# RWKV-7 and forgetting-attention layer: one recurrence operation for two heads, scores in quadrants, the inverse placed by 0/1 columns, and lo parts on VectorE

## Chip, cores and metric

The kernel runs on one core of one Trainium2 chip. The metric is the device time of one execution in microseconds, as the median of three runs. The engines are TensorE (PE in the profile, with its weight loads as PEld), VectorE (DVE), ScalarE (ACT), GpSimd (POOL) and SyncE (SP), which issues most of the DMAs.

## What is computed

One layer over 528 tokens (16 learned ones and 512 of the input) with 1024 channels. One projection of the normed input feeds three users: eight heads of the RWKV-7 delta rule, eight heads of forgetting attention, and two gates.

```python
u = rmsnorm(h, norm_mix[l])
proj = u @ w_in[l]
...
y_rw = rwkv7_branch(feat_rw, ...)   # S_t = S_{t-1} (diag(w_t) + a_t^T b_t) + v_t^T k_t ;  y_t = S_t r_t
y_fx = fox_branch(feat_fx, ...)     # softmax(q k^T * scale + F_q - F_k, causal) v
merged = gates[..., :D_MODEL] * (y_rw @ w_out_rw[l]) + gates[..., D_MODEL:] * (y_fx @ w_out_fx[l])
h = h + (merged @ w_o[l]).astype(h.dtype)
z = rmsnorm(h, norm_mlp[l])
h = h + (jnp.square(jax.nn.relu(z @ w_up[l])) @ w_down[l]).astype(h.dtype)
```

## The kernel before

**Products in two parts.** Large matrices are multiplied in three passes. Each 128 x 512 float32 weight block `wraw` is split into `whi`, a cast to float32r by ACT, and `wlo`, the difference `wraw - whi`. PE then forms hi*hi, hi*lo and lo*hi into one accumulator.

**Stages.** From the start to about 45 us the input is normed and the small projections run. From there to about 462 us run, interleaved, the 40 remaining blocks of the input projection (`projections`, matmuls L497), the recurrence (`Pair`, `inverse`, `chain`, `group_norm`) and attention (`fox_features`, `attention`). Then follow the output projections and the MLP. The change lies in the interleaved stage.

**Order of the work.** In that stage PE's order is written by a planner. `Turns` holds streams (Python generators) with ranks: 0 for `chain`, 1 for `recurrent`, 2 for `attention`, 3 for `fox_features`, 4 for `group_norm`, 8 for `projections`. A stream yields a time at which its operands are due; the first in rank whose due time plus a reserve (`ROOM`, 0.0 us for rank 0 and 0.8 for rank 1) is reached gets PE next, and `projections` fills what is left. Due times come from `Clock`, which books every instruction on its engine at a fixed price plus a rate per column (DVE 0.18 us + 1.06 ns, POOL 0.30 us + 2.1 ns). The order of DVE, ACT and POOL is made by the framework's scheduler from program order and priorities; each engine then works its list in that order. So PE stands still where an operand is later than the planner thought.

**Projections.** `convert` (L459) splits the next two halves of a weight block while the current one is multiplied. The cast is L466 on ACT, the difference L467 is on DVE for the first two blocks and on POOL after that. `wraw`, `whi` and `wlo` have four buffers each.

**The recurrence.** The eight heads are handled as four pairs; a pair's two heads lie on partitions 0-63 and 64-127 (`hss`). Two pairs make a group. Time is cut into 9 chunks of 64.

- `rows` builds for each head e a tile `L[e]` of 128 x 9 x 128. On the head's own 64 partitions stand the removal rows (columns 0-63: -kkn times the decay P, L753, and the first column of each chunk, L754) and the read rows (columns 64-127: r times P, L755).
- `scores` multiplies, per chunk and head, two of the three blocks of `BK` (b, k and a copy of b) with L (L784): weights of 64 x 128, so one matmul gives b's scores on the head's own 64 partitions and k's scores on the other 64. Every three chunks two PSUM banks (one for each head) are filled; DVE masks them into `Bm` (L787, own partitions) and into the other half of `L[e]` (L788).
- `inverse` inverts unit triangular 64 x 64 matrices: the 32 x 32 diagonal blocks of `Bm` are gathered into `Ain` by copies per partition quadrant (L821), transposed in blocks of 32, solved over 15 steps on DVE, transposed back, and placed by copies per quadrant (L845) into `Tt` and `Dn`, whose other 32 x 32 blocks are zeroed by POOL (L816, L840). Products of `Bm`, `Dn`, `W2` and `Tt` on PE (L851, 64 x 64 quadrants, both heads in one bank) complete it.
- `chain` then goes through the chunks: PE L911 gives Rs (copied by DVE L913), PE L917 with `Tt` gives the corrections (DVE L919), PE L932 the new state (DVE L934), PE L940 and L943 the outputs.
- `group_norm` (L221 and its neighbours are a reciprocal square root on 128 x 8) ends a half.

## Time and profile before

| | us |
|---|---|
| median of three runs | 889.76 (888.0 to 890.99) |
| the profiled execution | 888.58 |
| its span, first to last instruction | 886.8 |
| PE busy | 856.2 |
| DVE busy | 626.4 |
| ACT busy | 452.3 |
| POOL busy | 229.4, of which L467 has 103.7 in 76 operations |

A line of the profile names the source line, the engine, the operation, the tiles it writes and reads, the shape and the count; then come times, and in brackets or after a bar the idle time of the engine before it and what ended that. A busy PE is not PE at its peak, since matmuls are pipelined: two that start 0.23 us apart each show 0.39 us. The granted clock is TensorE's; 0.50 means that it ran at half speed.

### The profile page before, as it was taken

The page shows a single profiled execution, that of the slowest core. Times are in us where ns is not written, and L with a number is a line of the kernel's source. Part 1 is how long each engine was busy: PE and PEld are TensorE (multiplying, and loading weights), DVE is VectorE, ACT ScalarE, POOL GpSimd, SP SyncE. Part 2 cuts the span into 40 slices and gives each one's busy share as a digit, 9 for nine tenths or more (in the row PEclk, how much of TensorE's full clock was granted, in tenths as well). Part 3 has the DMA queues.
Part 4 walks back from the last instruction along what each step waited for, and adds up shares of the span by engine and source line. Part 5 has one row for each costly group of instructions (what it writes and reads, how often), then busy time and mean ns, then how long its engine had stood idle before and what let it go on. Part 6 is the DMA issues. An engine that isn't in the chain of part 4 may idle for free.

```text
span 886.8 us, 15663 instructions
## 1 busy us (share of the span) xinstructions
PE 856.2 (97%) x5896; PEld 698.0 (79%) x5896; DVE 626.4 (71%) x1186; ACT 452.3 (51%) x935; POOL 229.4 (26%) x201
## 2 busy tenths in 40 slices
PE   7889899999999999999989999999999999999998
PEld 6878887778896777677858788988888888888886
DVE  7975895547877883564377665587687777877787
ACT  7737333865465533665365563366445434544452
POOL 1154443222353351213102200210630171046000
PEclk9999999999999999999979999999999999999999
DMA  6121114021111231121256650472564175327331
GB/s 216 60 86 48 50 50 139 2 86 60 51 62 49 68 128 61 61 74 49 72 207 202 205 174 21 131 217 68 177 204 115 50 232 163 106 73 230 113 96 71
DMA packets 51339, 95.90 MB, mean 108 GB/s; under 512 B 5816, under 2 KB 6968, under 8 KB 51264
## 3 DMA queue, kind: packets, MB, share of 16 engines
q1 hardware_dynamic: 47680, 86.52, 30.4%
q0 software_dynamic: 1280, 4.20, 1.5%
q10 hardware_dynamic: 2304, 4.20, 1.3%
q8 instruction: 46, 0.75, 0.3%
q14 instruction: 29, 0.24, 0.1%
HBM read 88.57 MB, written 6.31 MB: 107 GB/s over the span
## 4 chain that ended last, share of the span: by engine, by line
PE 76%; DVE 11%; ACT 3%; DMA 3%; issue 2%; POOL 0%; ACTq 0%; DVEq 0%; POOLq 0%
PE pj L497 20%; PE po L1143 20%; PE po L1261 11%; PE pd L1261 5%; PE po L1113 3%; PE po L1064 2%; PE pw L851 1%; DMA gl<-gd 1%; PE psc L603 1%; PE py L648 1%; PE psr L784 1%; DVE L L755 1%; PE pbt L799 1%; PE pssq L549 1%; PE ppt L634 1%
## 5 line engine op out<-in xcount | busy, mean ns | idle before, releaser
L497 PE MATMUL pj<-uhi,whi 128*128 128x264 f32 (+1 forms) x480 | 167.6, 349 | 0.0
L497 PE MATMUL pj<-ulo,whi 128*128 128x264 f32 (+1 forms) x480 | 156.0, 325 | 2.4 <-DVE ulo L400 2.4
L497 PE MATMUL pj<-uhi,wlo 128*128 128x264 f32 (+1 forms) x480 | 155.6, 324 | 0.0
L467 POOL TENSOR_TENSOR wlo<-wraw,whi 128x512 fp32r<-128x512 f32 x76 | 103.7, 1368 | 194.9 <-ACT whi L466 180.8
L497 PEld LDWEIGHTS pj<-uhi,whi 128*128 128x128 f32 x480 | 91.6, 191 | 20.4 <-issue 11.3
L497 PEld LDWEIGHTS pj<-ulo,whi 128*128 128x128 f32 x480 | 92.1, 192 | 7.3 <-DVE ulo L400 3.0
L497 PEld LDWEIGHTS pj<-uhi,wlo 128*128 128x128 f32 x480 | 91.9, 191 | 7.1
L1143 PE MATMUL po<-zlo,whi 128*128 128x512 f32 (+1 forms) x248 | 94.9, 383 | 0.0
L1143 PE MATMUL po<-zhi,whi 128*128 128x512 f32 (+1 forms) x248 | 94.8, 382 | 0.0
L1143 PE MATMUL po<-zhi,wlo 128*128 128x512 f32 (+1 forms) x248 | 94.8, 382 | 0.0
L235 DVE TENSOR_TENSOR wlo<-wraw,whi 128x512 fp32r<-128x512 f32 x88 | 74.4, 856 | 27.8 <-ACT whi L234 27.7
L234 ACT CAST whi<-wraw 128x512 fp32r<-128x512 f32 x88 | 53.5, 617 | 48.3 <-DMA wraw<-in_wup 20.2
L1189 POOL TENSOR_TENSOR t<-traw 128x512 f32<-128x512 f32 x24 | 34.2, 1433 | 155.3 <-DVE wlo L270 138.9
L466 ACT CAST whi<-wraw 128x512 fp32r<-128x512 f32 x80 | 48.9, 617 | 42.0 <-PE pj L497 23.3
L1261 PE MATMUL po<-wlo,fhi 128*128 128x512 f32 x160 | 62.8, 392 | 0.2 <-DVE wlo L270 0.2
L270 DVE TENSOR_TENSOR wlo<-t,whi 128x512 fp32r<-128x512 f32 x64 | 49.4, 784 | 18.9 <-ACT whi L269 18.0
L269 ACT CAST whi<-t 128x512 fp32r<-128x512 f32 x64 | 39.9, 623 | 44.5 <-DVE wlo L270 20.6
L1261 PE MATMUL po<-whi,flo 128*128 128x512 f32 x160 | 62.4, 390 | 0.0
L1261 PE MATMUL po<-whi,fhi 128*128 128x512 f32 x160 | 62.0, 389 | 0.0
L1143 PEld LDWEIGHTS po<-zhi,wlo 128*128 128x128 f32 x248 | 46.6, 188 | 9.1
L1143 PEld LDWEIGHTS po<-zhi,whi 128*128 128x128 f32 x248 | 46.6, 188 | 9.1
L1143 PEld LDWEIGHTS po<-zlo,whi 128*128 128x128 f32 x248 | 46.6, 188 | 8.9
(298 smaller groups left out, 1839.7 us busy)
## 6 DMA issues: line engine op xcount, KB each, us to landing
wraw<-in_win SPq DMA_DIRECT2D x84, 256.0 KB, 2.6
wraw<-in_wup SPq DMA_DIRECT2D x64, 256.0 KB, 3.3
wraw<-in_wdn SPq DMA_DIRECT2D x48, 256.0 KB, 2.6
traw<-in_wdn SPq DMA_DIRECT2D x48, 256.0 KB, 3.0
gd<-gt ACTq DMA_DIRECT2D x16, 256.0 KB, 2.0
wraw<-in_wout SPq DMA_DIRECT2D x16, 256.0 KB, 3.0
gl<-gd SPq DMA_DIRECT2D x16, 256.0 KB, 3.0
wraw<-in_wo SPq DMA_DIRECT2D x16, 256.0 KB, 3.0
```

The lines of the kernel that those rows point to most:

```text
L234: A.copy(hi, raw)
L235: low.tensor_tensor(lo, raw, hi.bitcast(F32), ALU.subtract)
L269: A.copy(hi, x)
L270: V.tensor_tensor(lo, x, hi.bitcast(F32), ALU.subtract)
L466: A.copy(hi, raw)
L467: low.tensor_tensor(lo, raw, hi.bitcast(F32), ALU.subtract)
L497: mm(po, a, b[:, k, a0:a1], start=n == 0, stop=n == 23)
L1064: mm(po, a, b[:, k, :], start=n == 0, stop=n == 11)
L1113: mm(po, a[:, k, 128 * i:128 * i + 128], b[:, k, :], start=n == 0, stop=n == 23)
L1143: mm(po[:, t0:t1], a, b[:, k, t0:t1], start=n == 0, stop=n == 23)
L1189: eng.tensor_tensor(t, sums[c, pair] if c in (T1, T2) else c, d, ALU.add)
L1261: mm(x[i], a[:, k, left, 128 * i:128 * i + 128], c, start=start and k == 0 and n == 0, stop=stop and k == n_pairs - 1 and n == 2)
```

## The change

- `rows`: L753, L754 and L755 run once over all 128 partitions into `L[0]`; ACT copies the second head's partitions from there to `L[1]`, in two copies.
- `scores`: for each chunk, four matmuls with 64 x 64 weights instead of two with 64 x 128. The first bank takes the b scores of both heads, each on its own partitions; the second takes the k scores of both, each on the other head's partitions. `Bm` is masked in one operation on 128 partitions, `L` in two on 64.
- `inverse`: a tile `even` of two 0/1 columns marks the even and odd quadrants of 32 partitions. `Ain` is formed as `Bm`'s left block times the first column plus its right block times the second; `Tt` and `Dn` are written in two operations each, source times column. The zeroing of `Tt` and `Dn` by POOL falls away.
- `convert`: the difference `wlo` is always on DVE. `Clock` books whatever is written to a tile named `wlo` on POOL, as before.

```diff
-            eng = str(x.engine).split(".")[-1]
+            eng = "Pool" if out.startswith("wlo") else str(x.engine).split(".")[-1]
...
+    even = cp.tile([128, 2], F32, name="even")
...
+        for qd in range(4):
+            for odd in range(2):
+                G.memset(even[32 * qd:32 * qd + 32, odd:odd + 1], float(qd % 2 == odd))
...
         def convert(job, raws):
-            low = V if len(converted) < 2 else G
+            low = V
...
-                self.L = []
-                for e, hs in enumerate(hss):
-                    l1 = rp.tile([128, NCH, 128], F32, name=f"L{e}", bufs=2)
-                    V.scalar_tensor_tensor(l1[hs, :, 1:64], kkn[hs, :, 1:64], -1.0, P[hs, :, 0:63], ALU.mult, ALU.mult)
-                    V.tensor_scalar(l1[hs, :, 0:1], kkn[hs, :, 0:1], -1.0, None, ALU.mult)
-                    V.tensor_tensor(l1[hs, :, 64:128], r3[hs], P[hs], ALU.mult)
-                    self.L.append(l1)
+                self.L = l0, l1 = [rp.tile([128, NCH, 128], F32, name=f"L{e}", bufs=2) for e in range(2)]
+                V.scalar_tensor_tensor(l0[:, :, 1:64], kkn[:, :, 1:64], -1.0, P[:, :, 0:63], ALU.mult, ALU.mult)
+                V.tensor_scalar(l0[:, :, 0:1], kkn[:, :, 0:1], -1.0, None, ALU.mult)
+                A.copy(l1[hss[1], :, :64], l0[hss[1], :, :64])
+                V.tensor_tensor(l0[:, :, 64:128], r3, P, ALU.mult)
+                A.copy(l1[hss[1], :, 64:], l0[hss[1], :, 64:])
...
-                    sps = [psm("psr").rearrange("p (a b) -> p a b", b=128) for e in range(2)]
+                    sb, sk = [psm("psr").rearrange("p (a b) -> p a b", b=128) for e in range(2)]
                     for j in range(3):
-                        for e, hs in enumerate(hss):
-                            mm(sps[e][:, j, :], BK[hs, c0 + j, e:e + 2, :].rearrange("p a b -> p (a b)"), L[e][hs, c0 + j, :], start=True, stop=True)
-                    for e, hs in enumerate(hss):
-                        os, sp = hss[1 - e], sps[e]
-                        V.tensor_tensor(Bm[hs, c0:c0 + 3, :], sp[hs, :3, :], bc(tmask[hs], 1, 3), ALU.mult)
-                        V.tensor_tensor(L[e][os, c0:c0 + 3, :], sp[os, :3, :], bc(tmask[os], 1, 3), ALU.mult)
+                        for sp, row, turn in ((sb, 0, 1), (sk, 1, -1)):
+                            for (e, hs), os in zip(enumerate(hss), hss[::turn]):
+                                mm(sp[os, j, :], BK[hs, c0 + j, row, :], L[e][hs, c0 + j, :], start=True, stop=True)
+                    V.tensor_tensor(Bm[:, c0:c0 + 3, :], sb[:, :3, :], bc(tmask, 1, 3), ALU.mult)
+                    for e, os in enumerate(hss[::-1]):
+                        V.tensor_tensor(L[e][os, c0:c0 + 3, :], sk[os, :3, :], bc(tmask[os], 1, 3), ALU.mult)
...
-            if g > 0:
-                for r0, r1 in low:
-                    G.memset(Tt[r0, :, :, 32:64], 0.0)
-            for qd in range(4):
-                rs_ = slice(32 * qd, 32 * qd + 32)
-                o = 32 * (qd % 2)
-                for pr_ in range(2):
-                    V.tensor_copy(Ain[rs_, :, NCH * pr_:NCH * pr_ + NCH].rearrange("p t n -> p n t"), Bms[pr_][rs_, :, o:o + 32])
+            for pr_ in range(2):
+                dst = Ain[:, :, NCH * pr_:NCH * pr_ + NCH].rearrange("p t n -> p n t")
+                V.tensor_scalar(dst, Bms[pr_][:, :, :32], even[:, 0:1], None, ALU.mult)
+                V.scalar_tensor_tensor(dst, Bms[pr_][:, :, 32:64], even[:, 1:2], dst, ALU.mult, ALU.add)
...
-            G.memset(Dn, 0.0)
             for dst, src in ((Tt2, TT), (Dn, At)):
-                for qd in range(4):
-                    rs_ = slice(32 * qd, 32 * qd + 32)
-                    o = 32 * (qd % 2)
-                    V.tensor_copy(dst[rs_, :, o:o + 32], src[rs_, :, :n2].rearrange("p t n -> p n t"))
+                for odd in range(2):
+                    V.tensor_scalar(dst[:, :, 32 * odd:32 * odd + 32], src[:, :, :n2].rearrange("p t n -> p n t"), even[:, odd:odd + 1], None, ALU.mult)
```

## The prediction

> **What bounds the kernel now.** I read the page's head first, then the stretches, the waits of PE, the clock, one place in order of time, and last the groups that the diff touches. The page's first lines:

> ```profile
> span 886.8 us, 15663 instructions
> PE 856.2 (97%) x5896; PEld 698.0 (79%) x5896; DVE 626.4 (71%) x1186; ACT 452.3 (51%) x935; POOL 229.4 (26%) x201
> ```

> PE is busy nearly always, so the kernel can gain only where PE waits, runs at half clock, or gets less work. Stretches show where (columns: length, busy of PE, PEld, DVE, ACT, POOL, granted clock, DMA):

> ```profile
> 45.00:440.00 395.00, 380.36 (x3613) 304.80 (x3614) 262.79 (x618) 198.37 (x488) 131.47 (x113) 0.98 0.20 67
> 440.00:462.00 22.00, 18.43 (x116) 12.50 (x117) 18.33 (x53) 14.82 (x39) 0.00 (x0) 0.77 0.45 157
> 462.00:887.00 425.00, 420.07 (x1926) 347.93 (x1924) 307.36 (x429) 204.06 (x338) 92.36 (x72) 1.00 0.45 141
> ```

> The change works in 45 to 440 us only. PE idles 14.6 us there (395.0 - 380.4), with DVE at 67% and POOL at 33%. What it waits for, in total over the kernel:

> ```profile
> PE ppt L632 <- DVE pe L619: 2.8, 4, 1.8
> PE psr L784 <- DVE L L755: 2.7, 2, 1.6
> PE psr L784 <- DVE tm L313: 2.6, 2, 1.3
> PE pw L851 <- DVE AX L845: 1.7, 1, 1.7
> PE pch L917 <- DVE Rs L913: 1.6, 1, 1.6
> PE psr L784 <- DVE BK L743: 1.6, 1, 1.6
> PE psr L784 <- DVE L L788: 1.5, 2, 1.2
> ```

> DVE is what comes late: before the scores (L784), the inverse (L851), the chain (L917). After such waits the clock is halved for a stretch (the 0.50 that stands before the DMA share):

> ```profile
> 60.77:64.18 3.41, 3.41 (x24) 2.76 (x21) 3.33 (x9) 0.00 (x0) 0.94 (x1) 0.50 0.45 153
> 98.31:101.73 3.42, 3.33 (x24) 3.14 (x25) 3.00 (x7) 0.00 (x0) 1.07 (x1) 0.50 0.49 155
> 210.95:214.37 3.42, 3.42 (x22) 3.13 (x20) 1.25 (x4) 1.49 (x4) 1.42 (x1) 0.50 0.01 2
> 330.42:333.83 3.41, 3.41 (x21) 2.15 (x19) 0.00 (x0) 1.21 (x2) 1.27 (x1) 0.50 0.22 79
> 449.89:460.13 10.24, 9.12 (x52) 6.00 (x52) 9.20 (x26) 6.45 (x16) 0.00 (x0) 0.50 0.60 223
> ```

> Each of the first four costs half its length, 1.7 us, 6.8 us together; the fifth is the end of the stage and costs 5.1. Why DVE is late is seen in order of time:

> ```profile
> 207.59 1.27 POOL L467 TENSOR_TENSOR wlo<-wraw,whi 128x512 fp32r<-128x512 f32 x1 [1.38 <-ACT whi L466]
> 207.69 1.19 DVE L221 TENSOR_TENSOR rsgw<-st,rsgy 128x8 f32<-128x8 f32 x1
> ...
> 210.25 0.29 DVE L913 COPY Rs<-pch 128x128 f32<-128x128 f32 x1
> ...
> 210.59 0.45 PE L917 MATMUL pch<-Rs,Tt 64*64 64x64 f32 x8 [1.64 <-DVE Rs L913]
> ```

> An operation on 8 elements takes 1.19 us because it ends with POOL's wlo. Rs stands behind it, PE waits 1.64 us, and the half-clock stretch at 210.95 follows. By line, the same operation has two durations (ns, min/median/max):

> ```profile
> L467 POOL TENSOR_TENSOR wlo<-wraw,whi x76: 1261/1289/1830, 45.0 to 427.6; 128x512 fp32r<-128x512 f32 x76
> L467 DVE TENSOR_TENSOR wlo<-wraw,whi x4: 674/680/694, 25.8 to 42.6; 128x512 fp32r<-128x512 f32 x4
> L221 DVE TENSOR_TENSOR rsgw<-st,rsgy x12: 164/167/1249, 206.5 to 421.6; 128x8 f32<-128x8 f32 x12
> L753 DVE SCALAR_TENSOR_TENSOR L<-okk,P x8: 741/912/1811, 52.4 to 279.8; 64x567 f32<-64x567 f32 x8
> L755 DVE TENSOR_TENSOR L<-orr,P x8: 739/1334/1837, 56.7 to 265.5; 64x576 f32<-64x576 f32 x8
> L821 DVE COPY Ain<-Bm x16: 423/442/1461, 66.8 to 294.9; 32x288 f32<-32x288 f32 x16
> L845 DVE COPY Tt<-TT x8: 649/1188/1766, 128.9 to 321.4; 32x576 f32<-32x576 f32 x8
> L845 DVE COPY AX<-AX x8: 645/1152/1706, 133.4 to 328.2; 32x576 f32<-32x576 f32 x8
> L787 DVE TENSOR_TENSOR Bm<-psr,cs x24: 539/552/560, 61.4 to 291.4; 64x384 f32<-64x384 f32 x24
> ```

> Operations between SBUF tiles stretch by up to the 1.3 us of a wlo; L787, which reads PSUM, never does. The wait under tm L313 is of the same kind; that memset only follows this pair of L755, whose end at 60.27 us is what the scores lacked:

> ```profile
> 56.69 3.58 DVE L755 TENSOR_TENSOR L<-orr,P 64x576 f32<-64x576 f32 x2
> ```

> **The lo parts, wlo to DVE.** 76 operations leave POOL and cost DVE 76 x 0.68 = 51.7 us, by the four that it does already. What it gets back where POOL no longer holds it, median less minimum times count: L753 8 x 0.17, L755 8 x 0.60, L845 8 x 0.54 + 8 x 0.51, L821 16 x 0.02, together 14.9 us; others like L221 come on top. On DVE a wlo takes a turn between the chain's steps, and waits for its cast on ACT with everything behind it: Rs, uv, masks. PE waits for Rs. The planner still books wlo on POOL, so PE's order does not allow for that. No DMA is added or moved; the wraw buffers come free some 0.6 us sooner after each cast, and SP's loads are not what PE waits for.

> **L, the masks, the inverse.** L753 and L755 go from 8 to 4 each: 4 x (0.74 + 0.74) = 5.9 us. The masks (L787, and L788 of the same count and shape) go from 48 to 36 operations: 12 x 0.55 = 6.6. Ain takes 8 operations for 16 (3.5 by 0.44), the placement of Tt and Dn 8 for 16 (5.2 by 0.65). That the new ones, on 128 partitions, last as long as the old on 32 or 64 is an estimate from L467 on 128 and L755 on 64, both near 0.7 us for some 550 elements; with a column as factor and strided reads, from 0.65 (as now) to 1.2 us (the held copies), and I take 0.65. DVE's sum: 262.8 + 51.7 - 14.9 - 21.2 = 278 us of 395; its load hardly moves, so not its load but who holds it decides. POOL's memsets of Tt and Dn go, eight tiny ones come before the stage; POOL is idle, so nothing. ACT gets 8 copies of one head's half of L, by the nearest row:

> ```profile
> L744 ACT COPY BK<-BK x4: 672/672/675, 56.8 to 283.3; 128x576 f32<-128x576 f32 x4
> ```

> at most 8 x 0.67 = 5.4 us, under PE's projections at ACT's 50%; the last lies before the scores of the second head. The path through L still shortens: six operations of 2 x (0.74 + 0.16 + 0.74) = 3.3 us (0.16 for the column, as L221) become 1.64 + 0.67 = 2.3.

> **The scores in quadrants.** 144 matmul records of 64x128 weights become 288 of 64x64, as long each. The rows for how many run at once:

> ```profile
> 64.38 0.94 PE L784 MATMUL psr<-L,BK 64*128 64x128 f32 x12
> ...
> 65.25 0.19 PEld L497 LDWEIGHTS pj<-uhi,whi 128*128 128x128 f32 x1
> ...
> 155.06 0.27 PE L851 MATMUL pw<-AX,Tt 64*64 64x64 f32 x2
> ...
> 207.57 0.28 PE L911 MATMUL pch<-uv,L 128*64 128x64 f32 x2
> ```

> ```profile
> L851 PE MATMUL pw<-AX,Tt x144: 217/219/268, 146.6 to 347.3; 64*64 64x64 f32 x144
> ```

> ```profile
> 155.06:155.81 0.75, 0.75 (x24) 0.75 (x26) 1.00 0.00 0
> ```

> Twelve records of scores take 0.87 us with the change of form (64.38 to 65.25). If four quadrants run at once, 24 take as long: nothing added. If two, up to 0.87 more in each of 12 groups: 10 us. L851 shows two diagonal quadrants together (two records of at least 0.217 us are over in 0.27), L911 two column halves of the same rows (two in 0.28); four at a time is not in the trace. I take 2 us, nearer the lower end, since every kind of pair that the trace holds overlaps; the upper end stays in the range. Both heads' B rows now share one bank. [...]

> **The sum.** Waits that the lock or the removed operations make: 2.7 + 2.6 + 1.7 + 1.6 + 1.6 = 10.2 us, bounds 0 to 10.2 (BK is written from SBUF tiles too, so I count it to the lock). I take 8, since wlo will now be late sometimes itself. L788's 1.5 I leave. Half clock: 0 to 6.8; I take 5, three of the four stretches. Against it scores +2 (0 to 10) and wlo ahead of chain and masks +4 (0 to 23, below). Net -7: the profiled execution, 888.58 us (span 886.8 and 1.8 around it), goes to 881.6. It stands 1.2 below the median of 889.76, so **882.5 us**.

> [...]

> **Rivals.**
> *The chain behind wlo (slower).* Where the chain runs, as many wlo start on POOL:

> ```profile
> 165.00:225.00 60.00, 0.00 (x0) 10.91 (x9) 0.97 0.18 59
> 362.00:416.00 54.00, 0.00 (x0) 10.54 (x8) 1.00 0.19 64
> ```

> If each of these 17 stands before Rs or uv with its whole length and the wait for its cast (0.68 + 0.67, a cast like L744's copy), PE stalls 23 us where I took 4: 882.5 + 19 = 901.5. It decides from a mean of 0.65 us per wlo (4 + 7 = 11 us / 17). For: the chain has rank 0, whose reserve is 0.0, so PE turns to Rs at the moment planned for it, and the planner does not see it. Against: three steps per chunk leave DVE free in between, and it takes 0.29 us for Rs.

> [...]

> *The end gives it back.* The recurrence comes earlier in PE's order, projections run out sooner, and attention of the last heads stands bare as in 440 to 462, which loses 3.6 idle and 5.1 by clock. Once more of this, +8.7: 891. For: that stretch has little projection left to fill it. Against: PE's work is the same, and gates have the last rank.

> *More than forecast.* All 10.2 and 6.8 go, L788's 1.5 too, and the end of the stage, freed of a late group norm, loses half of its 8.7: -23 + 2 = 869.

> *The placement is no cheaper.* At 1.2 us the 8 operations of Tt and Dn cost as much as now; L851's wait and its clock stretch (1.7 + 1.7) stay: 886.

> **Chances.** Forecast 45%, more 18%, placement 5%, the end 12%, the chain 14%, row halves 6%. A measurement here tells 0.3% (2.7 us) from no change: under 887.1 is faster, over 892.4 slower. Forecast, more, and half of placement give 66% faster; the end and the rest 14% same; chain and row halves 20% slower. The forecast's own range is 876 to 888; to leave out no more than 2 in 10 I go from 866 to 898.

> **What would show it.** After: no wlo on POOL; L753's, L755's and L845's successors near their minima; no wait for L, AX or Rs over 1 us; at most one halved stretch between 45 and 440; scores' 24 records in under 1.1 us. Wrong if PE waits for Rs or uv in most chunks with a wlo just before them on DVE, if scores take 1.7 us, or if the stage ends no earlier than 462.

## The result and the profile after

| | before | after |
|---|---|---|
| median, us (22 runs each) | 890.46 (886.67 to 894.0) | 883.15 (880.21 to 892.01) |
| ratio, 95% interval | 1 | 0.9923 (0.9909 to 0.9937) |
| the profiled execution, us | 888.58 | 884.7 |
| start of the output projections, us in the profile | 461.13 | 450.64 |
| the rest, from there to the end, us | 425.7 | 432.3 |

The change makes the kernel 0.8% faster, 7.3 us by the medians. The two profiled executions lie only 3.9 us apart, because that of before was 1.9 quicker than its median and that of after 1.5 slower. Line numbers have moved by 2 to 4: the lo parts are L471 now, the products of L L755 and L758, the scores L788, the masks L789 and L791, the placement L841, the chain L907 to L930, the output projection L1060.

The page's head of after:

```profile
span 882.9 us, 15881 instructions
PE 852.5 (97%) x6040; PEld 695.1 (79%) x6040; DVE 619.7 (70%) x1222; ACT 459.1 (52%) x943; POOL 122.1 (14%) x129
```

PE has 144 records more (the scores in quadrants) and is busy 3.7 us less. The stretches, first of before, cut where the stage ends, then of after (columns as in the prediction: length, busy of PE, PEld, DVE, ACT, POOL, granted clock, DMA):

```profile
45.00:462.00 417.00, 398.79 (x3727) 317.30 (x3727) 281.12 (x670) 213.19 (x526) 131.47 (x113) 0.97 0.21 71
```

```profile
45.00:440.00 395.00, 385.04 (x3820) 308.27 (x3820) 264.88 (x679) 211.00 (x515) 23.99 (x33) 0.99 0.21 65
...
45.00:450.50 405.50, 391.22 (x3875) 312.17 (x3873) 273.79 (x702) 218.53 (x534) 23.99 (x33) 0.99 0.22 69
450.50:883.00 432.50, 424.45 (x1928) 350.69 (x1928) 308.36 (x434) 206.12 (x342) 91.93 (x72) 0.99 0.46 143
```

The stage lasts 10.5 us less. PE's idle time in it falls from 18.2 (417.0 - 398.8) to 14.3 us, and its busy time from 398.8 to 391.2 although no product was taken away: most of that part is the clock, since five halved stretches cost 11.9 us in it before and those that are left cost 4.9 (estimates, half of each length; in the one at 450.79 products of 512 columns start 0.43 us apart, and 0.23 us apart after it). After the stage PE idles 8.0 us (432.5 - 424.5) where it idled 4.9, and runs some matmuls at half clock; 6.6 us are given back there.

What PE waits for in the stage of after (total, times, longest):

```profile
PE psr L788 <- DVE L L791: 3.2, 4, 0.8
PE psr L788 <- DVE Bm L789: 2.8, 4, 0.9
PE po L1060 <- ACT whi L235: 2.5, 1, 2.5
...
PE pch L913 <- DVE Rs L909: 1.0, 3, 0.6
PE pup L713 <- DVE L L791: 0.9, 2, 0.4
PE pbt L802 <- DVE L L791: 0.8, 2, 0.4
PE pch L907 <- DVE uv L930: 0.6, 1, 0.6
```

The waits for the products of L, for the memset that stood for one of them, for AX and for BK are gone (2.7 + 2.6 + 1.7 + 1.6 = 8.6 us before), and the one long wait for Rs has become three short ones. What is new are waits for the masks: 3.2 + 2.8 + 0.9 + 0.8 = 7.7 us, where the scores waited 1.5 for a mask before. Most of what was won at L is lost again one step later (6.2 of 8.6). By line (ns, min/median/max):

```profile
L471 DVE TENSOR_TENSOR wlo<-wraw,whi x80: 670/692/1708, 26.5 to 424.6; 128x512 fp32r<-128x512 f32 x80
L755 DVE SCALAR_TENSOR_TENSOR L<-okk,P x4: 750/750/1665, 53.9 to 268.6; 128x567 f32<-128x567 f32 x4
L758 DVE TENSOR_TENSOR L<-orr,P x4: 749/1300/1862, 56.3 to 255.5; 128x576 f32<-128x576 f32 x4
...
L760 POOL TENSOR_TENSOR sq<-orr,sg x4: 1304/1537/1832, 55.9 to 268.4; 128x512 f32<-128x512 f32 x4
...
L789 DVE TENSOR_TENSOR Bm<-psr,cs x12: 539/540/553, 61.3 to 278.4; 128x384 f32<-128x384 f32 x12
L819 DVE TENSOR_SCALAR Ain<-Bm,even x4: 494/503/517, 65.7 to 279.5; 128x288 f32<-128x288 f32 x4
L841 DVE TENSOR_SCALAR AX<-AX,even x4: 739/745/756, 127.4 to 306.4; 128x576 f32<-128x576 f32 x4
```

On 128 partitions the operations last as long as they did on 64 (medians: L789 0.540 us, L787 0.552), and nothing that places the inverse is held any more (L841 takes 0.723 to 0.756 us, L845 took 0.645 to 1.766). L755 and L758 still are, once (1.67 us) and twice (1.86 and 1.85), for 0.75 otherwise: POOL keeps operations of its own in the recurrence, and L760 (1.30 to 1.83 us) runs beside these three.

The new wait, in order of time (start, length, and in brackets the wait just before):

```profile
59.58 1.29 DVE L471 TENSOR_TENSOR wlo<-wraw,whi 128x512 fp32r<-128x512 f32 x2
59.74 1.54 PE L788 MATMUL psr<-L,BK 64*64 64x128 f32 x48
...
61.32 0.55 DVE L789 TENSOR_TENSOR Bm<-psr,cs 128x384 f32<-128x384 f32 x1
...
61.91 1.12 DVE L791 TENSOR_TENSOR L<-psr,cs 64x384 f32<-64x384 f32 x2
61.93 0.43 PE L788 MATMUL psr<-L,BK 64*64 64x128 f32 x4 [0.65 <-DVE Bm L789]
63.18 0.87 PE L788 MATMUL psr<-L,BK 64*64 64x128 f32 x20 [0.81 <-DVE L L791]
64.80 0.36 PE L713 MATMUL pup<-lhi,lw 64*128 64x264 f32 x1 [0.43 <-DVE L L791]
```

The scores of three chunks take 0.77 us here (48 records in 1.54), against 0.87 before, which points to four quadrants at once. The two pairs of banks are full at 61.28, and the masks that free them take 0.55 + 1.12 for each. So PE stands before the third, first 0.65 for the bank of the b scores and then 0.81 for that of the k scores. This is so in each of the four pairs of heads. PE was sent there too early: the planner books a 64 x 64 score matmul at 128 columns / 1200 = 0.107 us, 24 of them as 2.56 us, and so allows the masks more time than they have. The first mask is late as well. Two lo parts, which the planner books on POOL, and a product of 0.49 us (L318) stand before it on DVE until 61.28, while the first pair of banks is full at about 60.5. One or two lo parts stand there in three of the four pairs.

### The profile page after: what moved, and what is told of

Read it like the earlier page. It is cut to its first block, busy times and chain, and to the rows that moved or that the text cites. A ratio compares the mean times of both kernels' runs of the same rounds, so it can differ in the third digit from the quotient of the medians.

```text
span 882.9 us, 15881 instructions
## 1 busy us (share of the span) xinstructions
PE 852.5 (97%) x6040; PEld 695.1 (79%) x6040; DVE 619.7 (70%) x1222; ACT 459.1 (52%) x943; POOL 122.1 (14%) x129
## 4 chain that ended last, share of the span: by engine, by line
PE 82%; DVE 6%; DMA 3%; ACT 2%; issue 1%; POOL 0%; SPq 0%; DVEq 0%; ACTq 0%; POOLq 0%
PE pj L501 27%; PE po L1139 20%; PE po L1257 11%; PE pd L1257 5%; PE po L1109 2%; PE po L1092 2%; PE pw L847 2%; PE psc L607 1%; DMA gl<-gd 1%; PE pbt L802 1%; PE py L652 1%; DMA wraw<-in_wup 1%; DVE L L791 1%; DMA wraw<-in_wout 1%; PE pssq L553 1%
## 5 line engine op out<-in xcount | busy, mean ns | idle before, releaser
L501 PE MATMUL pj<-uhi,whi 128*128 128x264 f32 (+1 forms) x480 | 167.9, 350 | 0.0
L501 PE MATMUL pj<-ulo,whi 128*128 128x264 f32 (+1 forms) x480 | 156.5, 326 | 2.6 <-DVE ulo L401 2.6
L501 PE MATMUL pj<-uhi,wlo 128*128 128x264 f32 (+1 forms) x480 | 156.1, 325 | 0.0
L501 PEld LDWEIGHTS pj<-uhi,whi 128*128 128x128 f32 x480 | 92.3, 192 | 19.8 <-issue 11.1
L501 PEld LDWEIGHTS pj<-ulo,whi 128*128 128x128 f32 x480 | 92.8, 193 | 7.1 <-DVE ulo L401 3.0
L501 PEld LDWEIGHTS pj<-uhi,wlo 128*128 128x128 f32 x480 | 92.5, 193 | 7.1
L236 DVE TENSOR_TENSOR wlo<-wraw,whi 128x512 fp32r<-128x512 f32 x88 | 71.3, 821 | 35.0 <-ACT whi L235 34.5
L471 DVE TENSOR_TENSOR wlo<-wraw,whi 128x512 fp32r<-128x512 f32 x80 | 56.6, 713 | 38.2 <-ACT whi L470 37.2
```

What stands on the lines that cost most here:

```text
L236: low.tensor_tensor(lo, raw, hi.bitcast(F32), ALU.subtract)
L471: low.tensor_tensor(lo, raw, hi.bitcast(F32), ALU.subtract)
L501: mm(po, a, b[:, k, a0:a1], start=n == 0, stop=n == 23)
```

## The experiments

Unless said otherwise the edit is against the changed kernel. Each variant's order on PE is planned anew, so single effects don't add up; where the order stays the same, this is said. Medians of before in the four series of runs lay between 889.7 and 890.5; ratios are to the one of the same series.

### The lo parts back on GpSimd, in the same order

```diff
-            low = V
+            low = V if len(converted) < 2 else G
```

The planner books wlo on POOL in both, so PE's order is that of the changed kernel, instruction by instruction.

> The changed kernel with wlo back on GpSimd (first two blocks on VectorE, as before); TensorE's order is the same, since the planner books wlo on GpSimd in both. Lock theory (GpSimd's wlo holds VectorE's operations between SBUF tiles): the waits for L and AX and Rs come back, about 8 to 12 us, ratio to the kernel before 0.995 to 1.005. Rival (the gain comes from fewer VectorE operations, and wlo on VectorE costs time): as fast as the changed kernel or faster, ratio 0.985 to 0.992.

Measured: 895.24 us, ratio 1.0059 (1.0037 to 1.0081). The same order costs 12 us more with wlo on POOL. The longest of its new waits, the stretch 45 to 440, and one place in order of time:

```profile
PE psr L788 <- DVE Bm L789: 5.4, 3, 2.8
```

```profile
45.00:440.00 395.00, 377.31 (x3733) 302.46 (x3733) 235.95 (x586) 205.85 (x500) 123.65 (x109) 0.97 0.20 64
```

```profile
51.74 3.12 POOL L471 TENSOR_TENSOR wlo<-wraw,whi 128x512 fp32r<-128x512 f32 x2 [1.28 <-ACT whi L470]
52.07 1.65 DVE L755 SCALAR_TENSOR_TENSOR L<-okk,P 128x567 f32<-128x567 f32 x1
...
53.64 1.26 DVE L756 TENSOR_SCALAR L<-okk 128x9 f32<-128x9 f32 x1
```

PE idles 17.7 us where the change idles 10.0, and the clock is 0.97 for 0.99. About half of the 12 us is clock: by an estimate from the mean clock of each run, (1 - clock) x span, a median run loses 16 us to halved stretches here and 10 in the change. L755 takes 1.65 us and L756, on 9 columns, 1.26, while two wlo run on POOL; in the change their medians are 0.75 and 0.17. This lengthening of DVE's operations between SBUF tiles beside POOL's is all that "the lock" stands for here; by what mechanism one holds the other was not shown. What it costs DVE in all follows from its busy time over the whole kernel: 592.7 us in 1146 operations here, and 76 wlo of 0.69 more would make 645.1; the change has 619.7 in 1222, so DVE got 25.4 us back.

### Half of the lo parts on GpSimd

```diff
-            low = V
+            low = V if len(converted) % 2 == 0 else G
```

> The changed kernel with every second block's wlo on GpSimd, same TensorE order. Lock theory: half of the distance between the changed kernel and the one with all of wlo on GpSimd (12 us), so 887 to 891, ratio 0.996 to 1.001. Rival (load and queueing on VectorE count as well, so that the best lies between): at most 884, ratio under 0.993.

Measured: 894.18 us, ratio 1.0045 (1.0028 to 1.0062), again in the same order on PE. Half of POOL's wlo cost 11 of the 12 us, not half of them. So the price isn't so much per operation. The wait for Bm, which comes after L, is even longer than with all of them:

```profile
PE psr L788 <- DVE Bm L789: 7.1, 4, 2.8
```

That a few meetings with the path L, scores, masks make nearly all of the cost fits this row, but was not tried by itself.

### The lo parts on VectorE alone

The kernel before, with only these lines:

```diff
-            eng = str(x.engine).split(".")[-1]
+            eng = "Pool" if out.startswith("wlo") else str(x.engine).split(".")[-1]
...
-            low = V if len(converted) < 2 else G
+            low = V
```

> The kernel before with wlo on VectorE and the planner booking it on GpSimd; L, masks and inverse in their old form; TensorE's order nearly that of before. Lock theory: the blocked durations of L753, L755, L821 and L845 go to their minima, most of the gain is there, ratio 0.990 to 0.996. Rival (queueing behind wlo on VectorE; 52 us more work there without the savings): ratio 1.000 to 1.015, with TensorE waiting for Rs and uv.

Measured: 888.71 us, ratio 0.997 (0.9948 to 0.9993): much less than expected. So the move that is worth 12 us beside the other parts is worth 1.8 beside the old ones (890.5 and 888.7). The operations are freed, but the time isn't won:

```profile
L755 DVE TENSOR_TENSOR L<-orr,P x8: 742/756/1848, 53.4 to 259.5; 64x576 f32<-64x576 f32 x8
```

```profile
PE psr L784 <- DVE L L788: 5.3, 6, 1.2
```

The median of this product falls from 1334 to 756 ns. Then the scores wait 5.3 us for the masks (1.5 before). Here too the wait moved one step on. The profiled execution, 881.16 us, is the fastest of the twelve and the only one at a clock of 0.994; the others had 0.980 to 0.988, so a typical run loses more to halved stretches than these rows show.

### The planner told that the lo parts are on VectorE

```diff
-            eng = "Pool" if out.startswith("wlo") else str(x.engine).split(".")[-1]
+            eng = str(x.engine).split(".")[-1]
```

> The changed kernel, but the planner books wlo on VectorE, where it runs. If TensorE waits behind wlo because the plan does not see it, this order is better: ratio 0.985 to 0.990. If the chain hardly meets wlo, or the plan now leaves gaps for late operands, ratio 0.992 to 1.000.

Measured: 905.17 us, ratio 1.0157 (1.0127 to 1.0186), outside both expectations. The truer booking makes the order 22 us worse. Waits, and the place of the longest:

```profile
PE pw L847 <- DVE AX L841: 12.3, 2, 8.1
```

```profile
313.42 1.55 PE L847 MATMUL pw<-AX,Bm 64*64 64x64 f32 x24 [8.11 <-DVE AX L841]
```

PE stands 8.1 us before the inverse with no projection put there. Why the planner leaves none was not tried and stays open.

### The new form of one part undone

Three kernels take the changed kernel and put back the old lines of one part, as they stand in the diff: the scores and masks (L784 to L788 of before), L for each head (L753 to L755), the placement (L821 and L845).

> The changed kernel with scores and masks in the old form (two matmuls of 64x128 weights a chunk, one bank for each head, four mask operations). TensorE's order is planned anew. If the new form's gain in VectorE work is what it gives (6.6 us), slower than the changed kernel by 2 to 6 us, ratio to before 0.994 to 0.999. If the new form mainly brought the new wait before L788 (about 6 us of waiting, from a planner price that is twice too high for four quadrants at a time), as fast or faster, 0.985 to 0.992.

> The changed kernel with L built for each head on 64 partitions as before. VectorE has 6.6 us more, the path to the scores is about 1 us longer in each of four pairs, ACT has 5.4 us less. If that path counts, 2 to 5 us slower than the changed kernel (ratio 0.994 to 0.998); if TensorE's fill hides it, within 1.5 us (0.990 to 0.994).

> The changed kernel with the inverse's gathering and placement by copies per quadrant, and GpSimd's zeroing of Tt and Dn. VectorE has about 7 us more, on the recurrence's path twice 3.5 us. If that path counts, 2 to 5 us slower than the changed kernel (ratio 0.994 to 0.998); if TensorE's fill hides it, within 1.5 us (0.990 to 0.994).

| put back | median, us | ratio (95%) |
|---|---|---|
| nothing (the change) | 883.15 | 0.9923 (0.9909 to 0.9937) |
| old scores and masks | 877.71 | 0.9863 (0.9836 to 0.9889) |
| old L | 889.12 | 0.9974 (0.9945 to 1.0004) |
| old placement | 884.28 | 0.9921 (0.9893 to 0.9949) |

Each of these kernels has an order of its own, and the differences hold order and part together. So measured, the quadrants cost 5 us, L for two heads is worth some 5, and the placement nothing that can be told. With the old scores PE still waits for the masks:

```profile
PE psr L787 <- DVE L L791: 4.3, 6, 1.2
```

The kernel before had 1.5 us there, the change has 7.7 with the neighbours: part of that wait comes without the quadrants. Of the old L's 12 runs the three at a clock of 0.992 or more took 881.5 to 884.6, the other nine, at 0.974 to 0.987, 885.2 to 894.4: this points to the clock for most of what L is worth.

One more had both the old scores and the old placement, so only the lo parts and the new L were left.

> The kernel before with two parts of the change alone: wlo on VectorE (booked on GpSimd) and L of two heads in one operation; scores, masks and the inverse's placement in the old form. If the placement is worth about 1 us and the quadrants cost what the planner's price makes of them, as fast as the changed kernel with the old scores: ratio 0.985 to 0.990. If the parts only work together: 0.992 to 0.998.

Measured: 885.02 us, ratio 0.9935 (0.9914 to 0.9956). Beside the old scores the placement is thus worth some 7 us (885.0 - 877.7), in orders that differ.

### The score matmuls at half the price

```diff
-                    cost = n / 600 if big else n / 1200
+                    cost = n / 600 if big else n / 2400 if out.startswith("psr") else n / 1200
```

> The changed kernel, but the planner prices a score matmul at half (four quadrants at a time instead of two), since in the changed kernel TensorE comes to the third pair of banks some 0.7 us before the masks have freed them, twice in each of four pairs of heads (about 6 us of waiting). If that wait is the planner's price: the waits before L788 fall under 2 us, 3 to 6 us faster than the changed kernel, ratio 0.985 to 0.989. If the masks themselves are the bound, whatever the order: ratio 0.991 to 0.994.

Measured: 874.02 us, ratio 0.9808 (0.978 to 0.9835): 9 us better than the change. The computation is the same; only the planner's price for one kind of matmul is halved. 24 of them are then booked at 1.28 us, still above the 0.77 measured. Waits, the stretch, and the place of the first pair of heads:

```profile
PE psr L788 <- DVE L L791: 1.7, 3, 0.6
```

```profile
45.00:440.00 395.00, 388.13 (x3868) 307.49 (x3868) 269.42 (x699) 215.43 (x528) 24.28 (x34) 1.00 0.22 70
```

```profile
58.84 1.54 PE L788 MATMUL psr<-L,BK 64*64 64x128 f32 x48
60.30 0.50 PE L501 MATMUL pj<-uhi,whi 128*128 128x512 f32 x1
...
61.20 0.44 PE L788 MATMUL psr<-L,BK 64*64 64x128 f32 x4
```

A projection (L501) now stands where PE waited 0.65 us for Bm. The scores' 6.0 us of waits become 1.7, a wait of 1.0 us for Bm before L553 is new, and idle in 45 to 440 goes from 10.0 to 6.9. DVE still has two lo parts before the first mask (58.67 to 59.96); PE now has a projection to do meanwhile. This shows that the price sent PE there too early. It doesn't show that the waits make all of the 9 us: by the mean clocks of the two profiled executions, 0.988 and 0.994, some 5 us are clock, and the wait for gl at L1092, after the stage, went from 3.0 to 0.2.

### Two of the others again, in that order

In the first, wlo goes back to POOL (`low = V if len(converted) < 2 else G`), with PE's order as just above; in the second, the old placement comes back.

> The kernel with the halved score price and wlo back on GpSimd, TensorE's order unchanged by it. Lock theory: GpSimd's wlo costs about as much as in the changed kernel's order, 9 to 15 us, so 883 to 889 (ratio 0.992 to 0.999). If the 12 us there came from the badly priced scores, which left no reserve for late operands: under 5 us, at most 879.

> The kernel with the halved score price and the inverse's placement in its old form (copies per quadrant, zeroing by GpSimd). The placement was worth about 1 us in the changed kernel and 7 us beside the old scores. If the 1 us was because the wait before the scores hid it: 878 to 882, ratio 0.986 to 0.990. If it is worth little with any score order that fits, and the 7 us came from a less lucky order: 873 to 876, ratio 0.980 to 0.984.

Measured: 885.41 us, ratio 0.9942 (0.9922 to 0.9963), and 882.69 us, ratio 0.9909 (0.9874 to 0.9944). The lo parts on VectorE are worth 11.4 us here and 12 in the changed kernel, much the same in these two orders, but 1.8 beside the old parts. The placement is worth 8.7 us here, and nothing in the changed kernel. That the wait for the masks hid it there fits; since each of these orders was planned anew, it isn't shown. One row shows a part of its cost, a wait of the projections for a wlo that the kernel with the new placement doesn't have:

```profile
PE pj L501 <- DVE wlo L471: 4.3, 2, 2.8
```

### The first weights of the output projection earlier

The end of the stage, in the changed kernel:

```profile
450.64 0.68 PE L1060 MATMUL po<-yhi,whi 128*128 128x512 f32 x1 [2.48 <-ACT whi L235]
...
497.63 0.63 ACT L1055 ACTIVATE gl<-gl 128x512 f32<-128x512 f32 x1 [1.92 <-DMA gl<-gd]
...
500.15 0.50 PE L1092 MATMUL po<-whi,mhi 128*128 128x512 f32 x1 [2.73 <-DVE gl L1062]
```

PE waits 2.48 us for the first cast of the next weights, and later 2.73 for a gate product, which waits for ACT, which waits for a DMA. Against the kernel with half the price, where the wait for the cast is 1.9 us:

```diff
+        w0 = load_w(wout[0])
...
-            w = load_w(wout[m])
+            w = load_w(wout[m]) if m else w0
```

> The kernel with the halved score price, and the first weights of the output projection loaded and split ahead of the splits of y_rw and y_fx instead of behind them. If TensorE's wait of 1.9 us for that cast is a matter of ScalarE's order, it falls under 0.5 us and the time to 870 to 873 (ratio 0.977 to 0.981); if attention's end then waits for ScalarE instead, no faster than 873.5.

Measured: 872.71 us, ratio 0.9804 (0.9778 to 0.9831). The wait for the cast is gone, but 1.3 us against the kernel with the price alone is no difference that these runs can tell. It and that kernel beat both the kernel before and the change.

## Why the prediction was right, and where it wasn't

The forecast, 882.5 us, came within 0.7 of the median, 883.15, and its net of -7 is the 7.3 measured. (The terms as they stand make 882.8, 889.76 - 7; the text says 882.5.) That the number came so near is partly luck. The profiled executions, on which the terms rest, lie only 3.9 apart. Two terms, +2 for the scores and +4 for wlo, went wrong, though their 6 is close to the 6.2 us of new waits for masks. And two things that it did not book nearly cancel: 5.1 us won at the stage's end and 6.6 lost behind it.

**The lock.** Right: POOL's wlo held DVE's operations (L845 into AX: a median of 1.152 us in before, 0.686 with wlo moved alone), and moving it is worth 12 us and 11.4 in two orders. But that worth needs the other parts: by itself the move won 1.8 us. The waits that it named, 10.2 us, lost 8.6 at L, AX and BK and 0.6 at Rs: 9.2 where it took 8. It was wrong about L758: it expected minima for both products of L, and L758's median is still 1.30 us (0.75 twice, 1.85 and 1.86).

**Half clock in the stage.** Foreseen -5, at most one stretch left in 45 to 440. Two begin in it, so -3.4. The end of a third, which began at 41.19, reaches to 48.01 and costs another 1.5; in before its like lay from 40.29 to 43.70, ahead of the stage. The stretch of 10.24 us at the stage's end, which the forecast left in place, is gone as well: another 5.1 us.

**The scores: the step that failed.** "If four quadrants run at once, 24 take as long: nothing added", and 2 us were taken from a range of 0 to 10. PE's work rose by nothing (0.77 us for 0.87). But the prediction then left "L788's 1.5", the wait for the masks, as it was. It had noted that the planner doesn't see wlo on DVE; it did not ask what the planner thinks of the quadrants. That wait went to 7.7 us with its neighbours, and the quadrants cost 5 us as planned, while with half the price the kernel with quadrants takes 3.7 us less than that with the old scores (874.0 and 877.7). The old scores with a lower price of their own were not tried; they were booked too high as well, 12 at 1.28 us for 0.87.

**wlo ahead of chain and masks.** For the chain +4 was too much. Rs and uv hold PE up for 1.6 us in all (2.2 before), so the rival with 17 stalls, 901.5 us, fell: it decided from 11 us in the chain. For the masks what it names is there: in three of the four pairs a wlo stands just before the first of them, and Bm is waited for 2.8 us. How much of that is the lo parts' doing was not tried by itself. DVE is busy 264.9 us in 45 to 440, not 278: of the lock it got back 25.4 over the kernel, where the five lines of the sum held 14.9.

**Row halves in one bank.** The scores of the two heads, from partitions 0-63 and 64-127, now go to one bank, and the chances kept 6% for a loss by that. None showed: 24 records take 0.77 us, where 12 with 64x128 weights took 0.87.

**The placement.** Priced at 0.65, measured 0.745 us; Ain at 0.44, measured 0.50 where it is written first. No term hung on that. Its worth, which the forecast had inside the AX wait, came to nothing in the change and to 7 to 9 us in two faster orders.

**The end.** A rival of its own (+8.7, 12%), not in the forecast. The stage ends 10.5 us sooner by the profile and 6.6 of that are lost behind it: two stretches at half clock, at 450.79 and 501.99, that cost 1.7 each, and the wait of 2.73 at L1092, 6.1 together. The rival's reason, attention that stands bare for want of projections, isn't what the waits show (PE's longest in attention, for pe at L636, make 1.9 us in all; before, at L632, 3.9); the late cast of the next weights and the gates' loads are. Half of it is clock, which another run may not lose in the same place.

## What to carry to other kernels

When a part becomes faster, ask who has written down the old price: here a planner booked 2.56 us for matmuls that took 0.77 and sent PE to wait, and one number was worth more than the whole change. One engine can cost another more by making its operations longer than by its work (a 0.75 us operation on DVE took up to 1.86 beside one on POOL); moving a 1.3 us operation to the busier engine at 0.69 us paid 11 to 12 us of 885 beside the other parts, and 1.8 alone. Undo each part both in the change and in the repaired kernel: a part that was worth nothing in the one was worth 8.7 us in the other.

## What the hardware showed that was not expected

```profile
207.54:210.95 3.41, 1.77 (x23) 1.42 (x22) 3.20 (x8) 0.30 (x1) 1.27 (x1) 1.00 0.40 135
...
279.22:282.63 3.41, 2.63 (x15) 2.07 (x13) 3.35 (x5) 0.00 (x0) 1.81 (x2) 1.00 0.16 54
282.63:286.04 3.41, 2.44 (x20) 2.02 (x22) 1.88 (x4) 2.16 (x4) 0.47 (x1) 1.00 0.07 25
```

And of after, with the four halved stretches that begin in the stage or behind it:

```profile
61.67:65.08 3.41, 1.91 (x29) 1.35 (x30) 3.32 (x7) 0.00 (x0) 0.00 (x0) 1.00 0.38 145
...
65.08:68.50 3.42, 3.42 (x12) 2.60 (x10) 2.33 (x5) 2.14 (x3) 0.00 (x0) 0.50 0.00 0
...
99.21:102.63 3.42, 1.99 (x32) 1.49 (x33) 3.33 (x7) 0.00 (x0) 0.00 (x0) 1.00 0.39 149
102.63:106.04 3.41, 3.41 (x20) 3.29 (x18) 2.28 (x5) 0.64 (x2) 0.00 (x0) 0.50 0.02 5
...
225.50:228.92 3.42, 2.13 (x68) 1.68 (x62) 3.31 (x10) 0.00 (x0) 0.48 (x1) 1.00 0.38 129
...
273.30:276.71 3.41, 1.92 (x53) 1.44 (x52) 2.15 (x4) 1.19 (x3) 0.00 (x0) 1.00 0.25 64
...
447.37:450.79 3.42, 0.94 (x15) 0.70 (x11) 3.42 (x7) 3.42 (x8) 0.00 (x0) 1.00 0.65 255
450.79:454.20 3.41, 3.41 (x9) 2.60 (x10) 2.24 (x4) 1.37 (x3) 0.00 (x0) 0.50 0.91 287
...
498.57:501.99 3.42, 1.60 (x6) 1.04 (x7) 3.09 (x5) 1.23 (x3) 0.55 (x1) 1.00 0.23 65
501.99:505.40 3.41, 3.41 (x10) 2.64 (x9) 0.69 (x1) 2.30 (x3) 1.05 (x1) 0.50 0.48 147
```

A window with 1.77, 1.91, 1.99, 0.94 or 1.60 us of busy PE is followed by a halved one, and so are those ahead of the other four of before, with 0.97, 0.59, 1.70 and 1.42. One with 2.63, 2.44 or 2.13 is not, nor one with 1.92. So these two executions part the windows only roughly, between 1.9 and 2.1 us of a busy time in which the ends of matmuls are modelled; that the busy time is what decides was not tried. Between 45 and 870 us every other window of both executions holds more than 2.1. This is read from windows at full clock; when a halved stretch ends, these figures don't tell (that at 449.89 lasts three windows). In before the wait of 1.6 us for BK fell on the two windows about 282.63 and cost no clock; that of 1.64 us for Rs fell in the one before 210.95 and cost 1.7 us more. The window up to 65.08, ahead of a halved stretch, has waits of 0.65 (in part), 0.81 and 0.43 us in it and no longer one. That the same program differs by several us from run to run could come from where the grid falls; the runs with the old L above show only that time and clock go together (881.5 to 884.6 us at 0.992 or more, 885.2 to 894.4 at 0.974 to 0.987), and no run set the grid by itself.

**Scores in 64 x 64 quadrants, into two banks, take 0.032 us a record.** 48 score records of 128 columns take 1.54 us, 0.032 each; 24 records of 64 columns, in pairs, took 0.75 us in before, 0.031 each. Twice the columns at the same time per record points to twice as many at once, which is read from these spacings alone.
